# One PSUM pool instead of three, GpSimd's arithmetic on VectorE and ScalarE, and a new order in the last head and at the end

## The chip, the cores and the metric

The kernel runs on one core of a Trainium2 chip. The metric is the device time of one execution in microseconds (us), as the median of several runs. A profiled execution gives a trace as well, in which each instruction of each engine has a start and a duration. The engines are TensorE (PE; its weight loads are PEld), VectorE (DVE), ScalarE (ACT), GpSimd (POOL) and SyncE (SP), which only issues DMAs here.

## The reference

A decoder of two layers is run for one step, for a new sequence of 512 tokens and for 8 samples of 4 tokens each (544 columns in all, of width 1024). Layer 0 mixes with a short gated convolution, layer 1 with retention in 4 heads. All is in float32. Cut to what matters:

```
def swiglu(x, w_gate, w_up, w_down):
    return (jax.nn.silu(x @ w_gate) * (x @ w_up)) @ w_down

def retention_chunkwise(q, k, v, s0):          # chunks of 128 tokens
    def step(S, qkv):
        scores = jnp.einsum('bhid,bhjd->bhij', qc, kc) * decay
        inner = jnp.einsum('bhij,bhjv->bhiv', scores, vc)
        cross = jnp.einsum('bhid,bhdv->bhiv', qc, S) * cross_w[:, :, None]
        S_new = S * chunk_decay[:, None, None] + jnp.einsum('bhjd,bhjv->bhdv', kc * state_w[:, :, None], vc)
        return S_new, inner + cross

def trunk(x, ...):
    for i in range(DEPTH):
        h = rmsnorm(x, norm_mix[i])
        m, st = short_conv_mixer(...) if i % N_MIXERS == 0 else retention_mixer(...)
        x = x + m
        x = x + swiglu(rmsnorm(x, norm_ffn[i]), ffn_w_gate[i], ffn_w_up[i], ffn_w_down[i])
    return rmsnorm(x, final_norm), ...
```

In retention q and k are rotated by position, each head's output is normalized, multiplied with silu of a gate, and projected. The outputs are y and the states of both mixers.

## The kernel before

Activations lie with 128 features on the partitions and the 544 columns along the free side, in two halves of 272 (`HT`). So that TensorE can multiply at its faster type without losing float32 precision, each operand is split into a high and a low part: `split` (L180 on ScalarE writes the high part, L181 on VectorE subtracts it and leaves the low one). `project` (L167) then issues three matmuls for each tile of weights and half: high x high, low x high, high x low. The weights stream in through SP's queue into a pool of three buffers, and their split parts (`wh`, `wl`) into another of three.

The stages, with the places in the profile in us: the convolution (to 217), feed-forward 0 (217 to 592), retention with its four heads (595 to 1122) and feed-forward 1 (1122 to the end).

**Feed-forward.** The first two of eleven pairs of hidden tiles are plain products (`whole_pairs`). The others are `Job`s, one for the gate and one for the up side of a pair: `weights7` and `operands` form sums of quarter matrices, so that seven products (L422, 12 matmuls of 272 columns each) do the work of eight. The weight sums are L381 and L383 on GpSimd, L382 and L384 on VectorE; w, w2 and w4 are their buffers. A job holds three accumulators a, b and c; L482 on VectorE adds what `take` hands out (`c11`, `c22`, `c12`) to the partial sums in `g` and `u`. Product 3 goes into the same bank as product 5, so it can start only when the `c22` add has read that bank. Behind the up job the activations are multiplied (L581 on VectorE, L583 and L585 on GpSimd) and split (`xh`, `xl`). The order within a job is 1, then 6, 5, 2, 7, then the next job's 1, then 4 and 3. Three pairs make a group; behind it `down` multiplies with eight pieces of the third matrix and `residual` (L251) adds into `x`. A scheduler fills matmuls of the next job between the pieces of `down`.

**PSUM.** There are eight banks of 512 columns. The convolution and feed-forward 0 have a pool of eight single banks, retention one of two tiles of two banks (`mm`) with four single banks (`sm`), feed-forward 1 again one of eight. A new pool can be used only when the old one's last reader is through.

**Retention.** `qk_first` forms q and k of the first head, `qk_rotate` rotates (L812 to L817; L814 and L815 on GpSimd), `gated` normalizes and transposes (`yn` L970, transposes L987, product L990) and `out_project` splits the gated values (`yh`, `yl`) and multiplies them with eight output tiles. The next head's q and k products fill in while a head is finished; the last head has none, and `rest` there delays the second half of the columns.

**The end.** The last three tiles of x (`LATE`) are done half by half: `products(hf)`, then `scaled(hf)`, which forms the column statistics (L684 with `sqacc` and `sqlast`), `rN` (L209, L210), a diagonal (L690, L691), its product with ones (L693), the copy R (L694) and the outputs `ya` and `yb` (L698 to L701), and stores them. The sums of squares are `square_sum`: L204 on ScalarE, L205 on GpSimd, the last one L201.

Of the kernel before, what the change touches and what calls it, by code (L numbers as in the profile page):

```python
# [10 lines left out]
ALU = mybir.AluOpType  # L11
# [25 lines left out]
SKIP0 = 6  # L37

# [9 lines left out]
def hybrid_decode_kernel(ctx: ExitStack, tc: tile.TileContext, a: dict, o: dict):  # L48
# [19 lines left out]
    def bank1():  # L68
        return ps[0].tile([P, 512], F32, tag="mm", name=nm("mm"))

    def phase(stack, name, tiles, banks=2, skip=0):
        ps[:] = stack.enter_context(tc.tile_pool(name=name, bufs=tiles, space=bass.MemoryType.PSUM)), banks
        for _ in range(skip):
            bank1()
# [181 lines left out]
    c01 = ExitStack()  # L256
    phase(c01, "ps0", 8, 1, SKIP0)
# [113 lines left out]
    def weights7(src1, src2, sw):  # L371
# [9 lines left out]
        nc.gpsimd.tensor_tensor(s1, a21, a22, op=ALU.add)  # L381
        nc.vector.tensor_sub(s2, s1, a11)  # L382
        nc.gpsimd.tensor_tensor(a21, a11, a21, op=ALU.subtract)  # L383
# [20 lines left out]
    class Job:  # L404
# [23 lines left out]
        def begin(self):  # L428
            self.a = bank1()[:, :HT]
            self.product(self.a, 1, True)  # L430
            self.take("u1", self.a)

        def middle(self):
            for which in (5, 6) if self.lead else (6, 5):
# [3 lines left out]
                else:  # L438
                    self.c = bank1()[:, :HT]
                    self.product(self.c, 5, True)  # L440
            self.b = bank1()[:, :HT]
# [46 lines left out]
    def ffn(layer, next_gain):  # L488
        with ExitStack() as c1:
            if layer == 1:  # L490
                phase(ctx, "ps3", 8, 1, 4)
# [29 lines left out]
            def whole_pairs():  # L521
# [4 lines left out]
                for m in range(WHOLE):  # L526
# [20 lines left out]
                    for q in range(2):  # L547
                        d = tp.tile([P, 2, T], F32, tag="gu", name=nm("gu"))
                        gu.append(d)
                        for i in range(2):  # L550
                            each(lambda p, di, r: nc.vector.tensor_mul(di, p, r), pts[q][i], halves(d[:, i, :]), R)
                            if q == 0:
                                nc.scalar.activation(d[:, i, :], d[:, i, :], AF.Silu)
                            else:
                                nc.gpsimd.tensor_tensor(d[:, i, :], d[:, i, :], gu[0][:, i, :], op=ALU.mult)
# [5 lines left out]
            def gate_up(m):  # L561
# [16 lines left out]
                def up(what, src):  # L578
# [57 lines left out]
            made_in = MADE if layer == 0 else list(range(KT))  # L636
            whole = whole_pairs()
            groups = [list(range(m, min(m + GROUP, HJ))) for m in range(0, HJ, GROUP)]
# [15 lines left out]
            late = LATE if layer == 1 else 0  # L654
            down(last, made_in[: KT - late])
# [3 lines left out]
    def final(ms, acts, group_weights, fp, tp):  # L659
# [4 lines left out]
        def products(hf):  # L664
            c = slice(hf * HT, (hf + 1) * HT)
            for n in range(KT - LATE, KT):
                wh, wl = ws[n - KT + LATE]
                pt = [None, None]
                pt[hf] = bank1()
# [5 lines left out]
        def scaled(hf):  # L675
# [3 lines left out]
            pt = bank1()  # L679
# [38 lines left out]
    c01.close()  # L718


    with ExitStack() as c2:
        phase(c2, "ps2", 2)
        p1 = c2.enter_context(tc.tile_pool(name="ps2s", bufs=4, space=bass.MemoryType.PSUM))

        def bank():
            return p1.tile([P, 512], F32, tag="sm", name=nm("sm"))

# [50 lines left out]
        def qk_first(st):  # L778
# [26 lines left out]
        def qk_rotate(st, which, dt, pt):  # L805
# [8 lines left out]
            nc.gpsimd.tensor_tensor(t0, r[:, 1, :], sin, op=ALU.mult)  # L814
            nc.gpsimd.tensor_tensor(r[:, 1, :], r[:, 1, :], cos, op=ALU.mult)  # L815
# [84 lines left out]
        def state(h, st):  # L900
# [4 lines left out]
            for dt in range(2):  # L905
# [6 lines left out]
            for dt in range(2):  # L912
# [16 lines left out]
        def gate_project(h, st, n):  # L929
# [8 lines left out]
            nc.gpsimd.tensor_scalar_mul(g, g, g_ret(h * 4 + n))  # L938
# [109 lines left out]
        def out_project(h, st, rest=None):  # L1048
# [6 lines left out]
            def split_half(c):  # L1055
# [3 lines left out]
            if rest is None:  # L1059
                split_half(slice(0, T))  # L1060
            else:
                split_half(slice(0, HT))
            for n2 in range(4):
                wh, wl = load_piece(a["rtout"][h, n2], 2 * 4 * P)
                if n2 == 0 and rest is not None:
                    pts = [psum() for _ in range(2)]
                    for hf in range(2):
# [186 lines left out]
```

## Time and profile before

| | us |
|---|---|
| median of 3 runs | 1527.51 (1526.33 to 1528.83) |
| profiled execution | 1527.99 |
| its span, first to last instruction | 1525.9 |
| TensorE busy | 1482.7, 11008 matmuls |
| VectorE busy | 939.5, 1342 instructions |
| ScalarE busy | 550.1, 792 instructions |
| GpSimd busy | 340.7, 266 instructions |
| mean granted clock of TensorE | 0.993 |

A row of a timeline gives the start, the duration, engine, line, operation, output <- inputs and shape, the number of instructions taken together (xN), and in brackets the idle time ahead of it with what ended it. A row of waits gives the total, how often and the longest. A row of a window gives the stretch, its length, the busy us of the five engines with the number of instructions, the granted clock, the DMA share and GB/s.

### The profile page before, as it was taken

What the parts mean: (1) busy time and instruction counts of PE and PEld (TensorE: products, weight loads), DVE (VectorE), ACT (ScalarE), POOL (GpSimd) and SP (SyncE); (2) the same over time, 40 slices, a digit from 0 to 9 for tenths busy, and PEclk for the clock granted to TensorE, in tenths of its full rate; (3) what the DMA queues carried; (4) which work ended last, traced back from release to release, by engine and by line L of the source; (5) the groups of instructions that cost most, each with busy time, mean ns of one, the idle gap of its engine ahead of it and who ended that gap; (6) DMA issues with size and microseconds to landing.
All of it is one profiled execution on the core that took longest, in us unless ns stands there. A gap on an engine that the chain in (4) does not pass through costs nothing.

```text
span 1525.9 us, 26206 instructions
## 1 busy us (share of the span) xinstructions
PE 1482.7 (97%) x11008; PEld 1397.0 (92%) x11008; DVE 939.5 (62%) x1342; ACT 550.1 (36%) x792; POOL 340.7 (22%) x266
## 2 busy tenths in 40 slices
PE   8999999999999998999999999999999999999997
PEld 7999999999999998897987988989699999999996
DVE  5645439848658546647536734735749848748554
ACT  5222355525425334231232222113265525425333
POOL 2000234304214112212102202201134313314113
PEclk9999999999999999999999999999999999999998
DMA  5222273223222226237235423713474223232222
GB/s 203 88 93 84 93 175 98 95 83 98 83 98 98 73 80 194 73 113 260 70 125 179 167 77 109 251 47 111 166 176 101 87 93 98 80 101 92 79 79 74
DMA packets 69462, 173.37 MB, mean 114 GB/s; under 512 B 6480, under 2 KB 22992, under 8 KB 69344
## 3 DMA queue, kind: packets, MB, share of 16 engines
q1 hardware_dynamic: 66432, 162.12, 32.0%
q0 software_dynamic: 2336, 8.46, 3.3%
q8 instruction: 86, 1.41, 0.4%
q10 hardware_dynamic: 576, 1.11, 0.2%
q14 instruction: 32, 0.26, 0.1%
HBM read 150.50 MB, written 21.18 MB: 113 GB/s over the span
## 4 chain that ended last, share of the span: by engine, by line
PE 76%; DVE 10%; issue 5%; POOL 4%; ACT 2%; DMA 1%; DVEq 0%; SPq 0%; ACTq 0%; POOLq 0%
PE mm L167 48%; PE mm L422 15%; DVE wl L181 3%; PE sm L838 2%; PE sm L839 2%; PE sm L840 2%; PE sm L1027 1%; ACT h L180 1%; DVE x L251 1%; PE sm L155 1%; PE sm L157 1%; DVE g L482 1%; POOL w L383 1%; POOL rot L815 1%; PE sm L156 1%
## 5 line engine op out<-in xcount | busy, mean ns | idle before, releaser
L180 ACT ACTIVATE wh<-w 128x1024 fp32r<-128x1024 f32 (+2 forms) x235 | 228.0, 974 | 515.1 <-PE mm L167 388.6
L167 PE MATMUL mm<-xh,wh 128*128 128x272 f32 x1760 | 373.6, 293 | 16.2 <-ACT wh L180 10.9
L167 PE MATMUL mm<-xh,wl 128*128 128x272 f32 x1760 | 367.0, 290 | 1.7 <-DVE wl L181 1.0
L167 PE MATMUL mm<-xl,wh 128*128 128x272 f32 x1760 | 364.6, 288 | 0.0
L181 DVE TENSOR_TENSOR wl<-w,wh 128x1024 fp32r<-128x1024 f32 (+2 forms) x235 | 294.3, 1257 | 39.9 <-ACT wh L180 38.5
L167 PEld LDWEIGHTS mm<-xh,wh 128*128 128x128 f32 x1760 | 276.8, 190 | 29.6 <-ACT wh L180 16.7
L167 PEld LDWEIGHTS mm<-xh,wl 128*128 128x128 f32 x1760 | 276.1, 189 | 4.7 <-DVE wl L181 4.3
L167 PEld LDWEIGHTS mm<-xl,wh 128*128 128x128 f32 x1760 | 277.4, 189 | 0.0
L251 DVE TENSOR_TENSOR x<-x,mm 128x272 f32<-128x272 f32 (+1 forms) x170 | 77.2, 487 | 199.1 <-PE mm L167 198.7
L422 PE MATMUL mm<-oh,wh 128*128 128x272 f32 x576 | 166.4, 289 | 0.0
L422 PE MATMUL mm<-oh,wl 128*128 128x272 f32 x576 | 166.3, 289 | 0.0
L422 PE MATMUL mm<-ol,wh 128*128 128x272 f32 x576 | 166.2, 289 | 0.0
L422 PE MATMUL mm<-oh,h 128*128 128x272 f32 x432 | 126.1, 292 | 6.5 <-DVE g L482 5.3
L422 PE MATMUL mm<-oh,l 128*128 128x272 f32 x432 | 124.8, 289 | 0.0
L381 POOL TENSOR_TENSOR w<-w 128x512 f32<-128x512 f32 x36 | 48.8, 1356 | 339.3 <-DMA w<-in_ffgu_dram 166.3
L422 PE MATMUL mm<-ol,h 128*128 128x272 f32 x432 | 124.5, 288 | 0.0
L422 PEld LDWEIGHTS mm<-oh,wh 128*128 128x128 f32 x576 | 108.6, 189 | 0.4 <-ACT u L479 0.4
L422 PEld LDWEIGHTS mm<-oh,wl 128*128 128x128 f32 x576 | 108.6, 189 | 0.0
L422 PEld LDWEIGHTS mm<-ol,wh 128*128 128x128 f32 x576 | 108.5, 188 | 0.0
L938 POOL TENSOR_SCALAR gate<-gate,vec 128x544 f32<-128x544 f32 x16 | 32.1, 2008 | 275.7 <-ACT gate L937 275.7
L181 DVE TENSOR_TENSOR l<-w,h 128x1024 fp32r<-128x1024 f32 x72 | 77.5, 1076 | 22.6 <-ACT h L180 21.9
L422 PEld LDWEIGHTS mm<-oh,h 128*128 128x128 f32 x432 | 81.4, 188 | 9.7 <-DVE g L482 7.5
(224 smaller groups left out, 2395.8 us busy)
## 6 DMA issues: line engine op xcount, KB each, us to landing
w<-in_ffgu_dram SPq DMA_DIRECT2D x88, 512.0 KB, 3.5
w<-in_ffdn_dram SPq DMA_DIRECT2D x96, 192.0 KB, 2.5
S<-in_rets_dram SPq DMA_DIRECT2D x16, 1024.0 KB, 7.3
out_rets_dram<-S SPq DMA_DIRECT2D x16, 1024.0 KB, 5.3
w<-in_cvin_dram SPq DMA_DIRECT2D x21, 512.0 KB, 3.5
w<-in_rtqk_dram SPq DMA_DIRECT2D x16, 512.0 KB, 3.5
w<-in_rtv_dram SPq DMA_DIRECT2D x16, 512.0 KB, 3.6
w<-in_rtg_dram SPq DMA_DIRECT2D x16, 512.0 KB, 4.0
```

Of the source, the lines that this page charges most:

```text
L155: nc.tensor.matmul(out, lh, rh, start=start, stop=False)
L156: nc.tensor.matmul(out, lh, rl, start=False, stop=False)
L167: nc.tensor.matmul(half(pt, hf)[:, :HT], w[:, c], act[k][:, hf * HT : (hf + 1) * HT], start=(first and k == ks[0] and i == 0), stop=(last ...
L180: nc.scalar.activation(dh, src, AF.Copy)
L181: nc.vector.tensor_sub(dl, src, dh.bitcast(F32))
L251: last_residual[0] = nc.vector.tensor_add(xk, xk, p)
L381: nc.gpsimd.tensor_tensor(s1, a21, a22, op=ALU.add)
L422: nc.tensor.matmul(out, w[:, c], b[k][:, at, :], start=(first and k == 0 and i == 0), stop=(k == n - 1 and i == 2), skip_group_check=True,)
L838: nc.tensor.matmul(out, xh[kt][:, ts_], wh[:, cw], start=(kt == 0), stop=False)
L839: nc.tensor.matmul(out, xh[kt][:, ts_], wl[:, cw], start=False, stop=False)
L840: nc.tensor.matmul(out, xl[kt][:, ts_], wh[:, cw], start=False, stop=(kt == KT - 1))
L938: nc.gpsimd.tensor_scalar_mul(g, g, g_ret(h * 4 + n))
```

## The change

One pool `ps` serves all phases: two tiles of two banks (`mm`, written m below) and four single banks (`sm`, written s; a pair of them makes one tile). `wide` sets in which order `psum()` hands out m and s. Jobs and statistics take single banks with `bank()`. L381, L383, L583, L585, the product in `whole_pairs` and two products of the rotation go from GpSimd to VectorE; the gate's scale goes to ScalarE. In the last head the state is formed in two halves of its rows (`dts`), the second one ahead of `out_project`, and the two gated steps are handed to it as a list. `out_project` cycles m, m, s. At the end the second half's products all stand ahead of the first half's outputs. Most lines behind L66 have a number that is one higher in the new kernel, and six lower from `qk_first` on (L251 is L252, L693 is L694, L987 is L981).

```diff
-    ps = [None, 2]
+    ps = ctx.enter_context(tc.tile_pool(name="ps", bufs=2, space=bass.MemoryType.PSUM))
+    kinds, at = ["m"], [0]
+    def wide(kind):
+        kinds[0], at[0] = kind, 0
     def psum():
-        if ps[1] == 1:
-            return [bank1(), bank1()]
-        return ps[0].tile([P, 2, 512], F32, tag="mm", name=nm("mm"))
+        kind = kinds[0][at[0] % len(kinds[0])]
+        at[0] += 1
+        if kind == "s":
+            return [bank(), bank()]
+        return ps.tile([P, 2, 512], F32, tag="mm", name=nm("mm"), bufs=2)
+    def bank():
+        return ps.tile([P, 512], F32, tag="sm", name=nm("sm"), bufs=4)
...
-        nc.gpsimd.tensor_tensor(s1, a21, a22, op=ALU.add)
+        nc.vector.tensor_add(s1, a21, a22)
         nc.vector.tensor_sub(s2, s1, a11)
-        nc.gpsimd.tensor_tensor(a21, a11, a21, op=ALU.subtract)
+        nc.vector.tensor_sub(a21, a11, a21)
...
                     elif what == "c22":
-                        nc.gpsimd.tensor_tensor(u[:, 1, HT:], u[:, 1, HT:], g[:, 1, HT:], op=ALU.mult)
+                        nc.vector.tensor_mul(u[:, 1, HT:], u[:, 1, HT:], g[:, 1, HT:])
                     elif what == "c12":
-                        nc.gpsimd.tensor_tensor(u[:, 0, :], u[:, 0, :], g[:, 0, :], op=ALU.mult)
+                        nc.vector.tensor_mul(u[:, 0, :], u[:, 0, :], g[:, 0, :])
...
+            wide("mmss")
             whole = whole_pairs()
+            wide("m")
...
             late = LATE if layer == 1 else 0
+            wide("mms")
             down(last, made_in[: KT - late])
...
         next(first)
-        next(second)
-        next(first, None)
         drain(second)
+        drain(first)
         drain(scaled(1))
...
-                    project(pt, wh, wl, 0, xh, xl, first, not first, ks=part, weave=iter(()) if first else steps)
+                    project(pt, wh, wl, 0, xh, xl, first, not first, ks=part, weave=iter(()) if first and pt is pts[0] else steps)
...
-            nc.gpsimd.tensor_tensor(t0, r[:, 1, :], sin, op=ALU.mult)
-            nc.gpsimd.tensor_tensor(r[:, 1, :], r[:, 1, :], cos, op=ALU.mult)
+            nc.vector.tensor_mul(t0, r[:, 1, :], sin)
+            nc.vector.tensor_mul(r[:, 1, :], r[:, 1, :], cos)
...
-            nc.gpsimd.tensor_scalar_mul(g, g, g_ret(h * 4 + n))
+            nc.scalar.activation(g, g, AF.Copy, scale=g_ret(h * 4 + n))
...
+            split_gated(slice(0, HT if rest else T))
+            wide("mms")
             for n2 in range(4):
                 wh, wl = load_piece(a["rtout"][h, n2], 2 * 4 * P)
+                pts = []
+                for n in range(2):
+                    pts.append(psum())
+                    if n2 == 0 and rest:
+                        rest[n]()
+                        project(pts[n], wh, wl, n * 4 * P, yh, yl, hfs=(0,))
+                    else:
+                        project(pts[n], wh, wl, n * 4 * P, yh, yl)
+                        residual(2 * n2 + n, pts[n])
...
-                        state(h, st)
+                        state(h, st, (0,))
...
             else:
-                out_project(h, st, rest)
+                state(h, st, (1,))
+                out_project(h, st, [lambda: gated(h, st, yn, 3), lambda: gated(h, st, yns, 4)])
```

The scheduler's order of instructions moves with it. VectorE, in the middle of a gate job of feed-forward 0, before (`mm_577` is the bank of products 5 and 3, the first add into it `c22`, the second `c12`):

```order
L482 TENSOR_TENSOR g_564_5094<-g_564_5094,mm_578_5179 128x272
L181 TENSOR_TENSOR wl_574_5146<-w_565_5127,wh_573_5145 128x1024
L482 TENSOR_TENSOR g_564_5094<-g_564_5094,mm_577_5166 128x272
L382 TENSOR_TENSOR w2_583_5252<-w2_583_5252,w_582_5251 128x512
L181 TENSOR_TENSOR wl_586_5261<-w_582_5251,wh_585_5260 128x1024
L181 TENSOR_TENSOR l4_576_5150<-w4_568_5130,h4_575_5149 128x512
L482 TENSOR_TENSOR g_564_5094<-g_564_5094,mm_577_5166 128x272
L384 TENSOR_TENSOR w4_584_5253<-w_582_5251,w2_583_5252 128x512
```

The same place on VectorE in the new kernel (the bank is `sm_533`, `c11` reads `sm_534`):

```order
L182 TENSOR_TENSOR wl_530_5064<-w_521_5045,wh_529_5063 128x1024
L482 TENSOR_TENSOR g_520_5012<-g_520_5012,sm_534_5097 128x272
L482 TENSOR_TENSOR g_520_5012<-g_520_5012,sm_533_5084 128x272
L381 TENSOR_TENSOR w2_539_5170<-w_537_5168 128x512
L382 TENSOR_TENSOR w2_539_5170<-w2_539_5170,w_538_5169 128x512
L383 TENSOR_TENSOR w_537_5168<-w_538_5169,w_537_5168 128x512
L182 TENSOR_TENSOR wl_542_5179<-w_538_5169,wh_541_5178 128x1024
L182 TENSOR_TENSOR l4_532_5068<-w4_524_5048,h4_531_5067 128x512
L482 TENSOR_TENSOR g_520_5012<-g_520_5012,sm_533_5084 128x272
L384 TENSOR_TENSOR w4_540_5171<-w_538_5169,w2_539_5170 128x512
```

The `wl` that stood between the `c11` and the `c22` add stands ahead of both, and L381 and L383 have come in behind them.

TensorE, in a down group of feed-forward 0 at the start of a new weight piece, before (`mm_637` and `mm_642` with their second halves are down pieces, `mm_627` is a bank of the next job):

```order
L167 MATMUL mm_637_5681<-xh4_82,wl_636_5678 128x272
L167 MATMUL mm_638_5682<-xh4_82,wl_636_5678 128x272
L422 MATMUL mm_627_5581<-oh_224_2270,l2_620_5515 128x272
L167 MATMUL mm_642_5728<-xh2_80,wh_640_5724 128x272
L167 MATMUL mm_643_5729<-xh2_80,wh_640_5724 128x272
```

And the new kernel's TensorE at the third piece of the same group (`mm_596` is the piece, `sm_583` and `sm_629` belong to the next job):

```order
L168 MATMUL mm_592_5597<-xl4_93,wh_590_5593 128x272 x2
L168 MATMUL mm_592_5597<-xh4_85,wl_591_5594 128x272 x2
L422 MATMUL sm_583_5499<-oh_201_2230,l2_576_5433 128x272
L422 MATMUL sm_629_5944<-oh_198_2227,h2_575_5432 128x272
L422 MATMUL sm_629_5944<-ol_202_2231,h2_575_5432 128x272
L422 MATMUL sm_629_5944<-oh_198_2227,l2_576_5433 128x272
L422 MATMUL sm_629_5944<-oh_199_2228,h2_575_5432 128x272
L422 MATMUL sm_629_5944<-ol_203_2232,h2_575_5432 128x272
L168 MATMUL mm_596_5642<-xh2_83,wh_594_5638 128x272 x2
```

Six matmuls of the job now stand where one stood, between the last use of one piece's weights and the first use of the next.

TensorE in the last head, before (`sm_1317` is attention output, L987 are transposes of `yn`, L167 the output projection):

```order
L155 MATMUL sm_1317_11002<-vh_1252_10550,sh_1269_10693 128x512
L156 MATMUL sm_1317_11002<-vl_1253_10551,sh_1269_10693 128x512
L157 MATMUL sm_1317_11002<-vh_1252_10550,sl_1270_10694 128x512
L987 MATMUL sm_1322_11024<-cb_64,yn_1313_10985 128x128 x4
L167 MATMUL mm_1332_11055<-yh_1327_11039,wh_1330_11050 128x272
L167 MATMUL mm_1333_11056<-yh_1327_11039,wh_1330_11050 128x272
L987 MATMUL sm_1334_11081<-cb_64,yn_1321_11022 128x128 x4
L987 MATMUL sm_1335_11087<-cb_64,yn_1326_11037 128x128 x3
```

The new kernel's TensorE ahead of the output projection (`mm_1274` is the second half of the state's rows):

```order
L156 MATMUL mm_1274_10919<-vh_1200_10445,knh_1187_10362 128x512
L157 MATMUL mm_1274_10919<-vl_1201_10446,knh_1187_10362 128x512
L158 MATMUL mm_1274_10919<-vh_1200_10445,knl_1188_10363 128x512
L168 MATMUL mm_1281_10951<-yh_1276_10935,wh_1279_10946 128x272
L168 MATMUL mm_1281_10951<-yl_1277_10936,wh_1279_10946 128x272
L168 MATMUL mm_1281_10951<-yh_1276_10935,wl_1280_10947 128x272
L168 MATMUL mm_1281_10951<-yh_1276_10935,wh_1279_10946 128x272
L981 MATMUL sm_1282_10952<-cb_67,yn_1268_10902 128x128 x4
```

Twelve matmuls of the state stand in place of the bare step from the transposes to the output projection.

More of the change, by code (lines that the diff above doesn't have):

```diff
@@ L428, in begin @@
         def begin(self):
-            self.a = bank1()[:, :HT]
+            self.a = bank()[:, :HT]
             self.product(self.a, 1, True)
@@ L668, in products @@
                 pt = [None, None]
-                pt[hf] = bank1()
+                pt[hf] = bank()
                 project(pt, wh, wl, 0, ah, al, hfs=(hf,))
@@ L678, in scaled @@
             yb = tp.tile([P, 4, HT], F32, tag="gu", name=nm("yb"))
-            pt = bank1()
+            pt = bank()
             mq = pt[:, 496:499]
@@ L711, in final @@
         next(first)
-        next(second)
-        next(first, None)
         drain(second)
+        drain(first)
         drain(scaled(1))
     ffn(0, lambda kt: g_mix(1, kt))
-    c01.close()
     with ExitStack() as c2:
[L722 to L726, printed above, removed]
+        wide("m")
         tp = c2.enter_context(tc.tile_pool(name="rt", bufs=2))
@@ L898, in keys, with state @@
             st["kn"] = (knh, knl, k2)
-        def state(h, st):
+        def state(h, st, dts=(0, 1)):
             knh, knl, k2 = st["kn"]
@@ L904, in state @@
             pt = psum()
-            for dt in range(2):
+            for dt in dts:
                 for jt in range(4):
@@ L911, in state @@
                     )
-            for dt in range(2):
+            for dt in dts:
                 so = tp.tile([P, DV], F32, tag="yn", name=nm("so"), bufs=2)
@@ L1053, in out_project, with split_gated @@
             yl = [yll[:, n, :] for n in range(4)]
-            def split_half(c):
+            def split_gated(c):
                 for n in range(4):
                     split(yh[n][:, c], yl[n][:, c], st["gate"][:, n, c])
[L1059 to L1062, printed above, removed]
+            split_gated(slice(0, HT if rest else T))
+            wide("mms")
             for n2 in range(4):
                 wh, wl = load_piece(a["rtout"][h, n2], 2 * 4 * P)
-                if n2 == 0 and rest is not None:
-                    pts = [psum() for _ in range(2)]
-                    for hf in range(2):
-                        if hf == 1:
-                            rest()
-                            split_half(slice(HT, T))
-                        for n in range(2):
-                            project(pts[n], wh, wl, n * 4 * P, yh, yl, hfs=(hf,))
+                pts = []
[7 more added lines that the diff above has]
+                        residual(2 * n2 + n, pts[n])
+                if n2 == 0 and rest:
+                    split_gated(slice(HT, T))
                     for n in range(2):
+                        project(pts[n], wh, wl, n * 4 * P, yh, yl, hfs=(1,))
                         residual(n, pts[n])
-                    continue
-                for n in range(2):
-                    pt = psum()
-                    project(pt, wh, wl, n * 4 * P, yh, yl)
-                    residual(2 * n2 + n, pt)
+            wide("m")
         st = qk_start(0)
@@ L1115, in hybrid_decode_kernel @@
                     else:
-                        state(h, st)
+                        state(h, st, (0,))
             yns = normalized(st["po"])
-            def rest():
-                gated(h, st, yn, 3)
-                gated(h, st, yns, 4)
             if more:
```

20 lines of the change are left out of this document (5 added, 15 removed).

## The prediction

> **What bounds the kernel now.** I read the page's busy times first, then the list of what TensorE waited for, then the timelines around each of those waits on the engine that is named.
>
> ```profile
> PE 1482.7 (97%) x11008; PEld 1397.0 (92%) x11008; DVE 939.5 (62%) x1342; ACT 550.1 (36%) x792; POOL 340.7 (22%) x266
> ```
>
> TensorE is busy for 1482.7 of 1525.9 us. The change issues the same matmuls, so a gain can come only from the 43.2 us in which TensorE sits idle, or from stretches in which its clock is low. The waits behind that idle time, on TensorE alone:
>
> ```profile
> PE mm L167 <- ACT wh L180: 10.9, 7, 7.5
> PE mm L167 <- DVE x L251: 7.1, 4, 4.0
> PE mm L422 <- DVE g L482: 5.3, 10, 1.0
> PE mm L693 <- DVE sqacc L691: 2.6, 2, 1.9
> PE mm L167 <- ACT yh L180: 2.5, 2, 1.7
> PE mm L684 <- POOL sqacc L205: 1.3, 1, 1.3
> PE mm L422 <- DVE u L482: 1.1, 2, 0.5
> PE mm L167 <- DVE wl L181: 1.0, 6, 0.2
> PE mm L167 <- ACT wh L185: 0.9, 1, 0.9
> PE sm L987 <- DVE yn L970: 0.9, 2, 0.6
> PE sm L238 <- DVE sqlast L233: 0.8, 1, 0.8
> PE mm L684 <- ACT sqlast L201: 0.7, 1, 0.7
> ```
>
> (Columns: total us, times, longest.) These rows add up to 35.1 us. 7.5 of them are the first load at the start, which the change does not touch; some 27.6 us in the middle are what it can win, and the tail behind the last matmul makes up the rest. I take the places one by one, by the kernel's stages.
>
> **A: the feed-forward jobs.** Product 3 adds into the bank that the `c22` add (L482) still has to read. It waits 5.3 + 1.1 = 6.4 us in twelve places. One of them:
>
> ```profile
> 472.29 2.19 DVE L181 TENSOR_TENSOR wl<-w,wh 128x1024 fp32r<-128x1024 f32 x1
> 472.11 1.29 POOL L381 TENSOR_TENSOR w<-w 128x512 f32<-128x512 f32 x1 [2.98 <-DVE l L181]
> 473.48 2.16 POOL L383 TENSOR_TENSOR w<-w,w 128x512 f32<-128x512 f32 x1
> 464.87 1.23 DVE L181 TENSOR_TENSOR wl<-w,wh 128x1024 fp32r<-128x1024 f32 x1 [0.16 <-ACT wh L180]
> 474.88 0.39 PE L422 MATMUL mm<-oh,h 128*128 128x272 f32 x1 [0.44 <-DVE g L482]
> ```
>
> The `c22` add stands on VectorE behind a `wl` subtraction. That instruction takes 1.23 us while GpSimd is silent, and 2.19 us while GpSimd runs L381 or L383: the two slow each other down. The costs for one gate and up pair of jobs (21.77 us), grouped:
>
> ```profile
> 460.12:481.89 21.77, 21.33 (x169) 21.11 (x168) 19.27 (x22) 11.83 (x20) 9.39 (x6) 1.00 0.32 111
> L181 DVE TENSOR_TENSOR wl<-w,wh 128x1024 fp32r<-128x1024 f32 x4 | 6.8, 1708 | 0.5 <-ACT wh L180 0.5
> L181 DVE TENSOR_TENSOR l<-w,h 128x1024 fp32r<-128x1024 f32 x3 | 3.7, 1225 | 2.3 <-ACT h L180 2.3
> L382 DVE TENSOR_TENSOR w<-w,w 128x512 f32<-128x512 f32 x2 | 2.9, 1428 | 0.0
> L384 DVE TENSOR_TENSOR w<-w,w 128x512 f32<-128x512 f32 x2 | 2.5, 1266 | 0.0
> L181 DVE TENSOR_TENSOR xl<-u,xh 128x544 fp32r<-128x544 f32 x2 | 1.4, 724 | 0.2 <-ACT xh L180 0.2
> L181 DVE TENSOR_TENSOR l<-w,h 128x512 fp32r<-128x512 f32 x2 | 1.4, 689 | 0.1
> L581 DVE TENSOR_TENSOR u<-mm,g 128x272 f32<-128x272 f32 x1 | 0.4, 428 | 0.0
> ```
>
> The first row is the window (TensorE, weight load, VectorE, ScalarE, GpSimd busy us); VectorE is at 19.27 of 21.77. The change puts six more instructions on it: L381 and L383 twice each, in the shape of the 689 ns row, so 4 x 0.69 = 2.76, and the two products at 0.43 and 0.72, together 3.91 us. What goes is the slowing down: wl 4 x (1.71 - 1.23) = 1.9, L382 2 x (1.43 - 0.69) = 1.5, L384 2 x (1.27 - 0.69) = 1.2, together 4.6 us. VectorE so ends at about 19.27 + 3.9 - 4.6 = 18.6 us a pair, against 169 x 0.126 = 21.3 us on TensorE: it stays the faster one. In the new order `c22` follows `c11` directly and the `wl` stands ahead of both, so the add is earlier by the whole subtraction, 1.2 to 2.2 us, and the longest wait was 1.0. New in VectorE's queue is that L381 waits for a weight load; L382 waited for the same pair of loads before, and behind GpSimd's 1.29 us, so nothing behind it comes later than now. I take 5.5 of 6.4 us; bounds 0 (the add stays behind something else) and 6.4. The rotations of retention lose GpSimd's two products each to VectorE at 0.72 each, and the gate's scale goes to ScalarE, which is busy 36%; both are covered by TensorE except in D.
>
> The Trainium skill, page "SBUF — State Buffer", section "Who interferes with whom", says that a VectorE instruction with two SBUF inputs contends with a GpSimd instruction that reads SBUF, and that the later one blocks completely until the other is done. The trace agrees that they contend, with a loss (0.96 us) smaller than either GpSimd instruction it met (1.29 and 2.16), so "completely" is not shown; by the full rule the saving would be up to 9.39 us a pair instead of 4.6, which changes nothing as long as TensorE is the longer.
>
> **B: the down groups.** At the start of each of six groups the second or third weight piece is split late:
>
> ```profile
> 519.52 0.84 ACT L180 ACTIVATE wh<-w 128x768 fp32r<-128x768 f32 x1 [5.25 <-PE mm L167]
> ```
>
> ScalarE was idle for 5.25 us and waited for a buffer that TensorE still read: of three buffers the next job holds two, and the matmuls of that job which fill in behind had run out (one single matmul is left ahead of the new piece). The waits: 10.9 - 7.5 = 3.4 us on `wh` and 1.0 on `wl`, 4.4 in all. With a single PSUM pool the down pieces use the two-bank tiles and the jobs the single banks, and the order has 6 job matmuls (0.75 us) for that one ahead of each of the next four pieces, and two ahead of the fifth. The waits on `wh` were 3.4 / 6 = 0.57 us each, so that is enough; for the last pieces it is not sure. I take 3.5; bounds 0 and 4.4.
>
> **C: into retention.** A new PSUM pool can be opened only when the last residual add has read the old one:
>
> ```profile
> 591.00 0.77 DVE L251 TENSOR_TENSOR x<-x,mm 128x272 f32<-128x272 f32 x2
> 594.62 0.77 DVE L251 TENSOR_TENSOR x<-x,mm 128x272 f32<-128x272 f32 x2
> 595.53 0.79 PE L167 MATMUL mm<-xh,wh 128*128 128x272 f32 x2 [3.98 <-DVE x L251]
> 595.50:601.50 6.00, 5.97 (x26) 6.00 (x27) 3.52 (x14) 1.22 (x2) 0.00 (x0) 0.50 0.90 295
> ```
>
> The first tile will need only the add of 591.00, the second that of 594.62, with 24 matmuls (3.0 us) between: 0.3 + 0.6 us stay of 3.98. The idle time has a second price: for six us behind it the granted clock is 0.50, and 26 matmuls take 5.97 us for 26 x 0.126 = 3.3, so 2.7 us more. The 0.8 on `sqlast` goes too, since the statistics start a half earlier; but two value matmuls instead of fourteen now cover the first rotation, which I put at 0.75 us. C: 4.0 + 2.7 + 0.8 - 1.7 = 5.8; bounds 2 (the clock still drops) and 7.5.
>
> The Trainium skill, page "TensorE: Matmul & The Clock Gate", part 1, says the clock halves after an idle window of about 3.4 us and needs a busy one to come back. The trace agrees here (3.98 us, then 0.50); in E below the clock falls with no single gap over 1.7 us, so there the trace is stricter than the rule. By the rule the gaps left in C keep the clock; by E's row they might not, which is the bound of 2.
>
> **D: the output projection** of heads 0 to 2 has two PSUM tiles, and the third product waits for a residual add:
>
> ```profile
> 735.59 0.72 DVE L817 TENSOR_TENSOR rot<-rot,rt 128x544 f32<-128x544 f32 x1 [1.25 <-POOL rot L815]
> 736.24 0.71 DVE L251 TENSOR_TENSOR x<-x,mm 128x544 f32<-128x544 f32 x1
> 737.00 0.52 PE L167 MATMUL mm<-yh,wh 128*128 128x272 f32 x2 [1.04 <-DVE x L251]
> ```
>
> The add stands in VectorE's order behind the end of a rotation that waits for GpSimd. Three such waits: 7.1 - 4.0 = 3.1 us. A third tile gives each add one more product (48 matmuls, 6 us), and the GpSimd step ahead of it is gone. I take 3.0; bounds 0 and 3.1.
>
> **E: the last head** has nothing to fill the gated products with: 2.5 us on `yh` and 0.9 on `yn`.
>
> ```profile
> 1092.90 0.78 PE L167 MATMUL mm<-yh,wh 128*128 128x272 f32 x2 [1.66 <-ACT yh L180]
> 1093.00:1097.00 4.00, 3.70 (x18) 3.31 (x19) 3.53 (x7) 0.81 (x3) 0.60 (x2) 0.58 0.11 41
> ```
>
> In the four us behind, the clock is 0.58: 3.70 x 0.42 = 1.55 us more. Half of the state's matmuls (12 at the 0.23 us of 512 columns, 2.8 us) move into the 1.66. The chain behind the last `yn` (transposes, gating, split) is then covered by nine matmuls only, 1.1 us, so I leave 1.2 standing: 3.4 + 1.55 - 1.2 = 3.7; bounds 1 and 4.9. Two state stores move with it behind SP's earlier work; nobody waits for them.
>
> **F: into the second feed-forward** goes the other new pool: 0.9 us, as its slot comes free a tile earlier; bounds 0 and 0.9.
>
> **G: the end.** All products of the second half now stand ahead of the first half's outputs:
>
> ```profile
> 1510.17 0.73 PE L693 MATMUL mm<-sqacc,ones 128*128 128x272 f32 x2 [0.76 <-DVE sqacc L691]
> 1512.19 1.72 DVE L701 SCALAR_TENSOR_TENSOR yb<-x,vec,mm 128x272 f32<-128x272 f32 x4
> 1513.68 0.38 PE L684 MATMUL mm<-cb,sqacc 128*128 128x1 f32 x2 [1.28 <-POOL sqacc L205]
> 1517.91 1.27 PE L693 MATMUL mm<-sqacc,ones 128*128 128x272 f32 x2 [1.86 <-DVE sqacc L691]
> ```
>
> The wait ahead of the first L693 is filled by one product (12 matmuls, 1.5 us from 1509.4), so the first half's L693 starts near 1510.9 for 1510.2. The sums for the second half on GpSimd, then ScalarE come ahead of the first half's outputs, so the second statistics need not wait for them and start near 1512.2 for 1513.7. But then `rN`, the next step, stands on VectorE behind six L701 (6 x 0.43 = 2.6 us from about 1511.8), so it is done near 1514.4; of the 1.5 won at the statistics and some 0.7 of waiting inside them, 1.7 stay. The half's output stores on ScalarE's and SP's queues move about 1 us back, and the second half's stand behind them. Bounds -2 (the two halves' outputs collide) and 2.5.
>
> **The sum**: 5.5 + 3.5 + 5.8 + 3.0 + 3.7 + 0.9 + 1.7 = 24.1 us. The profiled execution took 1527.99 us, 2.1 outside the span: 1525.9 - 24.1 + 2.1 = 1503.9, and as this execution stands 0.5 above the median of the runs (1527.51), I predict 1503.5.
>
> **Rivals.**
> 1. VectorE becomes the bound of the job pairs. This needs the slowing down not to come from GpSimd: then 19.27 + 3.91 = 23.2 us a pair stands against 21.3, 1.9 more for each of 18 pairs, 34 us lost against the 18.6 won outside A: about 1527.5 - 18.6 + 34 = 1543, slower. It decides from 21.3 + 18.6 / 18 = 22.3 us of VectorE a pair. Against it: 1.23 and 2.19 in the same instruction, by GpSimd's state. Chance 5%.
> 2. Half of it: A's and B's waits find another late producer (a weight load now at the head of VectorE's queue, one of four single banks not yet read), and 9.0 us stay: 1512.5. If C and E trip the clock again as well, 4 more: 1516.5. For it: 2.35 us of VectorE idle in a pair, on ScalarE, show that its order is tight. 20%.
> 3. The change does not do what it says: the banks' new split gives as many waits as it takes, in the whole pairs and the conv projection, which have few in the list now; 24 us come back, within 3 us (0.2%) of before, about what a measurement of this kernel can tell from no change. 6%.
> 4. All of the middle goes, and the clock's losses with it: 27.6 + 2.7 + 1.55 = 31.9 us, less 3 that the end keeps: 1498.5 and down to 1497. 7%.
>
> My own forecast, 1499 to 1510, has the remaining 62%. The range from 1498 to 1519 takes in rival 2 and leaves the two tails of 1 and 3. Faster 0.89, same 0.05, slower 0.06 by these cases.
>
> **What would show it.** A: no TensorE wait on L482 left, `wl` at 1.23 us throughout, VectorE at 18 to 19 us in a pair. B: no wait on `wh` over 0.2 us but the first. C: no gap over 1 us and a clock of 1.00 where retention starts. D: no residual add named by TensorE. E: two waits under 0.8 us near 1070 to 1080, clock over 0.9. G: the last L694 about 8.1 us behind the first half's statistics, for 10.3. Wrong it would be if a pair of jobs takes over 21.5 us, or if the list of waits names L381, L382 or the banks of L422.

## The result, and the profile after

The changed kernel takes 1492.06 us (median of 4 runs, 1491.29 to 1493.29) against 1527.72 of the kernel before on the same chip: a ratio of 0.9768, 95% interval [0.9751, 0.9785]. That is 35.7 us faster, where 24.1 were forecast; the time lies below the range. The direction and the places were right, the size was not.

The profile after has a span of 1490.7 us. Its busy times:

```profile
PE 1471.2 (99%) x11008; PEld 1392.7 (93%) x11008; DVE 919.5 (62%) x1400; ACT 565.9 (38%) x805; POOL 93.8 (6%) x118
```

And the list of what TensorE waited for (total us, times, longest):

```profile
PE mm L168 <- ACT wh L181: 6.7, 1, 6.7
PE sm L694 <- DVE sqacc L692: 2.4, 1, 2.4
PE sm L832 <- ACT wh L181: 0.9, 1, 0.9
PE sm L685 <- POOL sqacc L206: 0.8, 1, 0.8
PE sm L981 <- DVE yn L964: 0.6, 3, 0.2
PE mm L168 <- ACT yh L181: 0.5, 1, 0.5
PE mm L168 <- DVE x L252: 0.3, 1, 0.3
```

No L422 stands in it any more, and no `wh` but the first load's and one in the value product. TensorE issues the same 11008 matmuls, yet it is busy for 11.5 us less. The idle time fell from 43.2 us to 19.5, so it explains 23.7 of the 35.2 us of span; the rest is in the "busy" column.

To see where, the span is cut at the same matmuls of both traces, from start to start (us; the 9.0 forecast for A and B are put down half to each layer):

| stage | before | after | change | forecast |
|---|---|---|---|---|
| start to the first job matmul (L422) | 255.35 | 255.78 | +0.4 | 0 |
| first to last job matmul, layer 0 (A, B) | 312.46 | 302.05 | -10.4 | -4.5 |
| from there to the first value product (C) | 46.87 | 41.04 | -5.8 | -5.8 |
| first value products of head 0 to those of head 3 (D) | 397.66 | 393.94 | -3.7 | -3.0 |
| from there to the statistics of feed-forward 1 (E, F) | 116.75 | 113.13 | -3.6 | -4.6 |
| from there to the first job matmul | 44.31 | 44.31 | 0.0 | 0 |
| first to last job matmul, layer 1 (A, B) | 312.34 | 302.03 | -10.3 | -4.5 |
| last job matmul to the first end statistics | 20.66 | 20.66 | 0.0 | 0 |
| from there to the last product with ones (G) | 12.12 | 10.32 | -1.8 | -1.7 |
| tail | 7.41 | 7.41 | 0.0 | 0 |

All rows but those of the two job stages stand within 1 us of the forecast. The two job stages gave 20.7 us for 9.0: that is 11.7 us, the whole of the miss. The first row moves by up to 1.3 us between the traces (254.5 to 255.8 over all kernels here), and nothing is read from it.

VectorE in a pair of jobs, as the prediction reckoned it, first the window (another pair than the prediction's, of layer 0 too):

```profile
363.57:385.30 21.73, 21.73 (x175) 21.73 (x174) 18.26 (x28) 12.12 (x21) 0.00 (x0) 1.00 0.31 106
```

and the groups of instructions in it (count, busy us, mean ns of one, idle before):

```profile
L182 DVE TENSOR_TENSOR wl<-w,wh 128x1024 fp32r<-128x1024 f32 x4 | 4.9, 1222 | 0.9 <-ACT wh L181 0.9
L382 DVE TENSOR_TENSOR w<-w,w 128x512 f32<-128x512 f32 x2 | 1.4, 688 | 0.0
L381 DVE TENSOR_TENSOR w<-w 128x512 f32<-128x512 f32 x2 | 1.4, 682 | 0.0
L383 DVE TENSOR_TENSOR w<-w,w 128x512 f32<-128x512 f32 x2 | 1.4, 682 | 0.0
```

With GpSimd silent (0.00) `wl` takes 1222 ns for 1708 and L382 688 for 1428. VectorE holds more instructions than before and is busy for less: 18.26 us where 18.6 were worked out. TensorE has no idle time left in the window.

### The profile page after: what moved, and what is told of

It reads as the page before. It is cut to its first block, busy times and chain, and to the rows that moved or that the text cites. A ratio compares the mean times of both kernels' runs of the same rounds, so it can differ in the third digit from the quotient of the medians.

```text
span 1490.7 us, 25998 instructions
## 1 busy us (share of the span) xinstructions
PE 1471.2 (99%) x11008; PEld 1392.7 (93%) x11008; DVE 919.5 (62%) x1400; ACT 565.9 (38%) x805; POOL 93.8 (6%) x118
## 3 DMA queue, kind: packets, MB, share of 16 engines
q8 instruction: 86, 1.41, 0.4%
q10 hardware_dynamic: 576, 1.11, 0.2%
## 4 chain that ended last, share of the span: by engine, by line
PE 95%; DVE 3%; issue 1%; ACT 1%; POOL 0%; DMA 0%; DVEq 0%; SPq 0%; POOLq 0%; ACTq 0%
PE mm L168 43%; PE sm L422 26%; PE sm L168 11%; PE sm L832 2%; PE sm L833 2%; PE sm L834 2%; PE sm L1021 1%; PE sm L156 1%; PE sm L158 1%; PE sm L157 1%; PE mm L1034 1%; DVE wl L182 1%; PE mm L839 1%; PE mm L156 1%; PE sm L981 1%
## 5 line engine op out<-in xcount | busy, mean ns | idle before, releaser
L252 DVE TENSOR_TENSOR x<-x,mm 128x544 f32<-128x544 f32 x86 | 61.9, 720 | 170.1 <-PE mm L168 170.1
L422 PE MATMUL sm<-oh,wl 128*128 128x272 f32 x576 | 166.5, 289 | 0.0
L422 PE MATMUL sm<-oh,wh 128*128 128x272 f32 x576 | 166.5, 289 | 0.0
L422 PE MATMUL sm<-ol,wh 128*128 128x272 f32 x576 | 166.3, 289 | 0.0
L422 PE MATMUL sm<-oh,l 128*128 128x272 f32 x432 | 124.7, 289 | 0.0
L422 PE MATMUL sm<-ol,h 128*128 128x272 f32 x432 | 124.7, 289 | 0.0
L422 PE MATMUL sm<-oh,h 128*128 128x272 f32 x432 | 124.6, 288 | 0.0
L422 PEld LDWEIGHTS sm<-oh,wh 128*128 128x128 f32 x576 | 108.7, 189 | 0.4 <-ACT u L479 0.4
L422 PEld LDWEIGHTS sm<-oh,wl 128*128 128x128 f32 x576 | 108.7, 189 | 0.0
L422 PEld LDWEIGHTS sm<-ol,wh 128*128 128x128 f32 x576 | 108.5, 188 | 0.0
L182 DVE TENSOR_TENSOR l<-w,h 128x1024 fp32r<-128x1024 f32 x72 | 68.7, 955 | 35.7 <-ACT h L181 35.5
L422 PEld LDWEIGHTS sm<-ol,h 128*128 128x128 f32 x432 | 81.4, 188 | 0.0
L422 PEld LDWEIGHTS sm<-oh,l 128*128 128x128 f32 x432 | 81.4, 188 | 0.0
```

The lines of the kernel that those rows point to most:

```text
L182: nc.vector.tensor_sub(dl, src, dh.bitcast(F32))
L252: last_residual[0] = nc.vector.tensor_add(xk, xk, p)
L422: nc.tensor.matmul(out, w[:, c], b[k][:, at, :], start=(first and k == 0 and i == 0), stop=(k == n - 1 and i == 2), skip_group_check=True,)
```

## What was open

Theory 1: a wait costs more than the idle time that the profile shows for it. A matmul of 272 columns is shown for 0.29 us, but the next one starts 0.126 us behind it. So the first 0.163 us of any wait lie beneath the shown end of the matmul ahead, and shorter waits show nothing. Theory 2: with GpSimd silent, TensorE itself runs faster everywhere. Beside this, each step had its own question: whether it was the contention or the order on VectorE that made the waits of A, and whether the fall of the clock in C and E came from the waits.

The rows of the kernel before already had the answer, one wait of A on TensorE:

```profile
276.90 0.29 PE L422 MATMUL mm<-oh,wl 128*128 128x272 f32 x1
277.72 0.39 PE L422 MATMUL mm<-oh,h 128*128 128x272 f32 x1 [0.53 <-DVE u L482]
277.94 0.29 PE L422 MATMUL mm<-ol,h 128*128 128x272 f32 x1
278.07 0.29 PE L422 MATMUL mm<-oh,l 128*128 128x272 f32 x1
```

The starts are 0.82 and 0.22 us apart where 0.13 is the rule. The wait cost 0.69 + 0.10 = 0.79 us, and 0.53 are shown. The 0.10 is in the next spacing: the first matmul behind a wait is shown for 0.39 us instead of 0.29.

## The experiments

### e1: GpSimd's work moved, nothing else

In the kernel before:

```diff
-        nc.gpsimd.tensor_tensor(s1, a21, a22, op=ALU.add)
+        nc.vector.tensor_add(s1, a21, a22)
...
-            nc.gpsimd.tensor_scalar_mul(g, g, g_ret(h * 4 + n))
+            nc.scalar.activation(g, g, AF.Copy, scale=g_ret(h * 4 + n))
```

and likewise the other six that the change moves.

> The kernel before with GpSimd's sums and products moved to VectorE and ScalarE, and nothing else. Theory 1 (a wait of TensorE costs 0.16 us more than the idle time shown, since a matmul is shown for 0.29 us and the next can start after 0.126; waits under 0.16 us show no idle time at all): the twelve waits on c22 go with 6.4 us of idle time and 8.5 us of start-to-start time, perhaps 1 to 3 us in D; the down groups and the PSUM boundaries stay. 1516 to 1519 us, and the time between the first and last job matmul of a layer falls by 4.2 to 5.5 us of 312.4. Theory 2 (GpSimd's silence lets TensorE run faster everywhere): the whole unexplained 10 us of the two job stages comes with the moves: 1508 to 1511 us, and the usual spacing of matmuls falls below 0.1256 us.

Measured: 1512.45 us, ratio 0.9898 [0.9883, 0.9913], 15.9 us faster than before. The waits that stay:

```profile
PE mm L167 <- ACT wh L180: 10.1, 7, 6.7
PE mm L167 <- DVE x L251: 4.0, 1, 4.0
PE mm L167 <- ACT yh L180: 2.4, 2, 1.6
```

All twelve waits on L482 are gone, and the job stages take 307.17 and 307.19 us, 5.3 and 5.2 less: within theory 1's 4.2 to 5.5 and half of what theory 2 asks. The spacing of matmuls that wait for nothing stays at 0.126 us, where theory 2 wanted less. The total does not decide: it lies 3.6 us below theory 1's range and 1.5 above theory 2's. D gave more than the 1 to 3 us allowed for: of the four waits on the residual only the one of C is left, and the stage from head to head fell by 4.4 us. So GpSimd's moves alone take away D's waits, most likely its two products in the rotation, which the prediction's rows show ahead of the add; the third tile is not needed for that. B, E and F stay as they were.

Two more things differ. C takes 45.73 us for 46.87 and the end 13.11 for 12.12, though their waits are those of the kernel before: the same 3.98 us ahead of retention are followed by a mean clock of 0.72 over six us, where it was 0.50, and at the end the clock is 0.53 from 1498 to 1500 us, during the statistics, where it was 1.00 before. What a wait costs in clock so is not the same each time. And the scheduler's order moved along: in ten of the 18 gate jobs, the very ten that waited before, `c22` now follows `c11` directly, as in the new kernel. So e1 has both cures of A and cannot part contention from order.

### e2: one pool, the new last head and the new end, with GpSimd's work back

In the changed kernel, the edit of e1 the other way round.

> The changed kernel with all of GpSimd's sums and products put back on GpSimd; one pool, the last head and the end stay as changed. Theory 1: waits of the down groups stay gone; if the c22 waits come back, they cost 8.5 us start to start, so 1500 to 1504 us; if the order keeps c22 ahead of the weight sums, 1493 to 1497 us. Either way the loss equals the idle time shown plus 0.16 us a wait, plus short waits that show nothing. Theory 2: 1506 to 1510 us whatever the list of waits shows.

Measured: 1502.96 us, ratio 0.9837 [0.9821, 0.9853]. Eleven of the twelve waits of A are back. The list has three more rows that the kernel after lacks, of 0.2 to 0.4 us each; the rows of A are:

```profile
PE sm L422 <- DVE g L482: 4.8, 10, 1.0
PE sm L422 <- DVE u L482: 0.5, 1, 0.5
```

The job stages take 307.03 and 306.17 us. B's and D's waits stay gone, so the pool gives all of B: 5.4 and 6.2 us a layer against the kernel before, or 5.2 a layer as what e1 leaves of the whole, from a listed 4.4 us for both layers. In e2 and the kernel before alike the spacing of matmuls that wait for nothing is 0.126 us, as in the kernel after, and the time lies in theory 1's range, 3 us under theory 2's. Theory 2 falls: GpSimd's silence did not make TensorE's matmuls come closer together.

### e3 and e6: half of GpSimd's work back

e3, in the changed kernel:

```diff
-        nc.vector.tensor_add(s1, a21, a22)
+        nc.gpsimd.tensor_tensor(s1, a21, a22, op=ALU.add)
...
-        nc.vector.tensor_sub(a21, a11, a21)
+        nc.gpsimd.tensor_tensor(a21, a11, a21, op=ALU.subtract)
```

> The changed kernel with only the two weight sums L381 and L383 back on GpSimd. VectorE's wl goes back to 1.7 us on average and L382 and L384 to 1.3 to 1.4. If the contention made the c22 waits (my prediction's step A), they come back: 1500 to 1503 us. If it was the place of c22 in VectorE's order (here it still follows c11 directly), the 1.2 us of slack cover the contention: 1491.5 to 1494 us. Theory 2: about 1500 us with no waits to show for it.

e6, in the changed kernel:

```diff
-                        nc.vector.tensor_mul(u[:, 1, HT:], u[:, 1, HT:], g[:, 1, HT:])
+                        nc.gpsimd.tensor_tensor(u[:, 1, HT:], u[:, 1, HT:], g[:, 1, HT:], op=ALU.mult)
...
-                        nc.vector.tensor_mul(u[:, 0, :], u[:, 0, :], g[:, 0, :])
+                        nc.gpsimd.tensor_tensor(u[:, 0, :], u[:, 0, :], g[:, 0, :], op=ALU.mult)
```

> The changed kernel with only the two products behind the up job (c22 and c12 with the gate) back on GpSimd; the weight sums stay on VectorE. Its order on VectorE has a wl subtraction between the c11 and the c22 add again. If c22's place in the order makes the waits on product 3: six a layer come back, 4.2 us a layer start to start, 1499 to 1502 us in all. If contention made them: GpSimd has two short instructions a pair only, 1492.5 to 1494.5 us.

Measured: e3 1493.84 us (0.9777 [0.9763, 0.9792]), e6 1491.72 us (0.9767 [0.9753, 0.9782]), which is the changed kernel's time and 0.8 us below the lower of e6's two ranges. VectorE at the same gate job, first of e2, then of e6, then of e3:

```profile
366.43 0.43 DVE L482 TENSOR_TENSOR g<-g,sm 128x272 f32<-128x272 f32 x1
366.77 2.17 DVE L182 TENSOR_TENSOR wl<-w,wh 128x1024 fp32r<-128x1024 f32 x1
368.88 0.42 DVE L482 TENSOR_TENSOR g<-g,sm 128x272 f32<-128x272 f32 x1
```

```profile
363.57 0.43 DVE L482 TENSOR_TENSOR g<-g,sm 128x272 f32<-128x272 f32 x1
363.92 1.22 DVE L182 TENSOR_TENSOR wl<-w,wh 128x1024 fp32r<-128x1024 f32 x1
365.05 0.43 DVE L482 TENSOR_TENSOR g<-g,sm 128x272 f32<-128x272 f32 x1
```

```profile
363.55 2.31 DVE L182 TENSOR_TENSOR wl<-w,wh 128x1024 fp32r<-128x1024 f32 x1
365.79 0.77 DVE L482 TENSOR_TENSOR g<-g,sm 128x272 f32<-128x272 f32 x2
```

In e2, as before, both the contention (2.17) and the bad order (`wl` between `c11` and `c22`) are there, and TensorE waits. e6 has the bad order without contention: no wait, 302.09 and 302.05 us. e3 has the contention without the bad order in this job (both adds in one row, behind `wl`): 302.85 and 303.21 us. It is the same in all ten gate jobs that waited: `wl` stands between the two adds in each of them in e6, in none of them in e3. So there a wait needed both, and either cure suffices nearly alone. Neither of the two single causes that I set against each other, in e3 and in e6, was the whole of it. e3 also shows short waits that nearly escape the view: the stages are 0.8 and 1.2 us longer, and no L422 stands in its list of waits, which leaves out idle times of up to 0.15 us.

### e4 and e5: a late first tile in retention

e4 asks for a tile at the start of retention and leaves it (one line, `psum()`); e5 writes one column of it, which nobody reads:

```diff
+            skipped = psum()
+            nc.tensor.matmul(half(skipped, 0)[:, :1], ident, mean_w[:, 0:1], start=True, stop=True)
             pts = [psum() for _ in ws]
```

> The changed kernel with one PSUM tile skipped at the start of retention, so that the first product waits for the last residual add (584.9 us in the profile after) instead of the one before it. Idle time of about 3.3 us comes back there. If the clock falls behind it as in the kernel before (0.50 for 6 us): 2.7 us more, in all +5.6 us: 1497.7 us. If the clock's fall has nothing to do with the wait: +3.0 us: 1495.0 us, clock 1.00.

> The changed kernel, in which one PSUM tile at the start of retention is written with one column that nobody reads, so that the first product gets the tile whose last reader is the last residual add (at 584.2 to 584.9 us in the profile after). About 3.3 us of idle time come back there (3.5 start to start), less the 0.5 that the second tile waited. If the clock falls behind it, as the prediction's step C has it: 2.5 to 2.7 us more, 5.6 us in all: 1497.7 us and a clock near 0.50 for some 5 us. If the clock's fall in the kernel before had another cause: +3.0 us, 1495.1 us, clock 1.00.

Measured: e4 1491.61 us (0.9761 [0.9747, 0.9776]), with the trace of the changed kernel at that place: a tile that is never written holds no one up, and the run says nothing on the clock. e5: 1494.19 us (0.9784 [0.9769, 0.9798]), and stage C takes 44.27 us for 41.04. The wait that came is another than I meant, statistics ahead of the products, and at 1.95 us it is shorter than the 3.3 I planned, so the time is below both of my figures; but a wait is there. TensorE's row in the timeline, then the windows behind it:

```profile
583.00 0.38 PE L225 MATMUL sm<-cb,sqacc 128*128 128x1 f32 x2 [1.95 <-POOL sqacc L206]
```

```profile
584.00:586.00 2.00, 2.00 (x13) 2.00 (x13) 2.00 (x12) 1.30 (x2) 0.00 (x0) 0.67 0.86 277
586.00:588.00 2.00, 2.00 (x11) 2.00 (x10) 1.80 (x4) 0.00 (x0) 0.00 (x0) 0.50 0.89 307
```

Eleven products run at full clock behind it, and only then, 1.4 us after the first of them, the clock falls to 0.50 for about 3.4 us: fifteen matmuls stand 0.227 us apart for 0.126, which is 1.5 us of the 3.2 lost. With the tile free in time the clock stays at 1.00 there, so the clock's part of C was a price of the wait, as step C had it.

### e7 and e8: the last head and the end

e7 forms the last head's state whole, as before; e8 has the old order of the end:

```diff
-                        state(h, st, (0,))
+                        state(h, st)
...
-                state(h, st, (1,))
```

```diff
         next(first)
+        next(second)
+        next(first, None)
         drain(second)
-        drain(first)
```

> The changed kernel with the last head's state formed whole, where the kernel before formed it, so that nothing stands between the last attention product and the output projection. By the prediction's step E: about 2 us of idle time and 0.3 to 0.5 of hidden time come back, and the clock falls again for 2 to 4 us (1 to 1.5 us): +3 to +4 us, 1495 to 1496 us. If the list of two gated steps and the order around it, not the state's twelve matmuls, made the gain: within 1 us of the changed kernel.

> The changed kernel with the end in the old order (one product of the second half behind the first half's outputs). By the prediction's step G: +1.8 us between the first statistics and the last product with ones, 1493.9 us. If the gain there came from the other parts: no difference.

Measured: e7 1493.64 us (0.9778 [0.9761, 0.9794]), e8 1493.64 us (0.9779 [0.9765, 0.9794]). In e7 the last head's stage takes 115.67 us for 113.13, and the clock falls again there, 0.50 in one window of two us:

```profile
1072.00:1074.00 2.00, 0.40 (x3) 0.30 (x2) 1.53 (x7) 0.79 (x3) 0.61 (x2) 0.98 1.03 382
1074.00:1076.00 2.00, 1.54 (x8) 1.15 (x8) 2.00 (x4) 0.60 (x2) 0.43 (x1) 0.50 0.15 56
```

That is 2.5 us, less than the 3 to 4 I expected but well over the other case's 1, and most of the 3.6 that E and F gave: the state's twelve matmuls are most of it. In e8 the end takes 12.11 us for 10.32: 1.8, as expected to a tenth. Both medians, 1.6 us above the changed kernel's, lie inside the interval of the ratio; it is the stage times of the traces that carry these two readings.

### e9: waits of known size

Behind the changed kernel's last output stand rounds of one matmul, whose result ScalarE copies for the next round, and m more that don't depend on it (`fresh` is a copy on ScalarE, `stretch(t, m)` issues m matmuls, `HT` is 272):

```diff
+        for m in range(10, 0, -1):
+            for r in range(12):
+                d = bank()
+                nc.tensor.matmul(d[:, :HT], xh[0][:, :P], t, start=True, stop=True)
+                nxt_t = fresh(d[:, :HT], 1e-3)
+                stretch(t, m)
+                t = nxt_t
...
+        for k in range(1, 10):
+            d = bank()
+            nc.tensor.matmul(d[:, :HT], xh[1][:, :P], t, start=True, stop=True)
+            t = fresh(d[:, :HT], 1e-3)
+            for _ in range(k - 1):
+                t = fresh(t.bitcast(F32))
+            stretch(t, 96)
```

> The changed kernel, with a measurement of its own behind its last output (its time is that much longer, some 350 us). Part 1: 12 rounds each of one matmul, whose result ScalarE copies to be the next round's operand, and m further matmuls behind it, m from 10 down to 1, all 128x272 on TensorE. With a chain of about 0.9 us, TensorE must wait for less and less time as m grows. Theory 1 (idle time shown is the true wait less 0.16 us): at each m the time of a round is (m+1) x 0.126 plus the idle time shown plus 0.16 us, and there is an m (6 or 7) at which rounds are longer than (m+1) x 0.126 with no idle time shown. Theory 2 (idle time shown is the whole wait): a round is (m+1) x 0.126 plus the idle shown. Part 2: stretches of 96 matmuls (12 us) parted by one wait behind k ScalarE copies, k from 1 to 9, so waits of about 0.7 to 3.5 us. If the clock falls behind a wait as short as the 1.9 us of e5, it stays 1.00 up to k = 3 or 4 and is 0.50 for about 3.4 us behind longer ones, not always at the same length; if only waits of over 3 us count, up to k = 7.

Measured (a profiled execution, 1785.15 us with the addition): the chain from one such matmul to the next is 0.88 us. TensorE's rows for m = 6, then 4, then 3:

```profile
1568.01 0.29 PE L1147 MATMUL sm<-t,xh 128*128 128x272 f32 x1
1568.14 0.92 PE L1140 MATMUL sm<-t,xh 128*128 128x272 f32 x6
1568.90 0.28 PE L1147 MATMUL sm<-t,xh 128*128 128x272 f32 x1
...
1589.06 0.39 PE L1147 MATMUL sm<-t,xh 128*128 128x272 f32 x1
1589.29 0.66 PE L1140 MATMUL sm<-t,xh 128*128 128x272 f32 x4
1589.94 0.39 PE L1147 MATMUL sm<-t,xh 128*128 128x272 f32 x1
...
1600.50 0.40 PE L1147 MATMUL sm<-t,xh 128*128 128x272 f32 x1
1600.74 0.54 PE L1140 MATMUL sm<-t,xh 128*128 128x272 f32 x3
1601.39 0.39 PE L1147 MATMUL sm<-t,xh 128*128 128x272 f32 x1
```

All three rounds take 0.88 us. With seven matmuls that is 7 x 0.126, and nothing is lost. With five, 0.63 us of work takes 0.88, and no idle time is shown at all: rows touch, the next one starting at 1589.94 where the shown ones end at 1589.29 + 0.66 = 1589.95. With four, 0.38 us is lost and 0.11 shown (1600.74 + 0.54 = 1601.28 to 1601.39). The medians over the rounds:

| m | work (m+1) x 0.1256 | round | lost | idle shown | difference |
|---|---|---|---|---|---|
| 6 | 0.879 | 0.879 | 0.00 | 0 | 0 |
| 5 | 0.754 | 0.880 | 0.13 | 0 | 0.13 |
| 4 | 0.628 | 0.881 | 0.25 | 0 | 0.25 |
| 3 | 0.502 | 0.880 | 0.38 | 0.11 | 0.27 |
| 2 | 0.377 | 0.881 | 0.50 | 0.24 | 0.27 |

So theory 1 holds, with a larger figure than I gave it: a wait costs 0.27 us more than it shows, 0.16 beneath the end of the matmul ahead and 0.105 in the longer spacing behind. The chain alone sets the length of these rounds, so the table shows how much loss goes unseen; that the longer spacing costs the kernel itself time is seen from its own spacings, below. (At m = 1 the granted clock is 0.68; that row is left out.)

In part 2 the waits are 0.55, 1.01, 1.41, 1.87, 2.33, 2.79, 3.25, 3.71 and 4.17 us of idle time. The first five leave the clock alone; the last four are followed by 16, 15, 12 and 24 matmuls at 0.227 us for 0.126. The bound so lies between 2.33 and 2.79 us here, between the two cases that I had set; each length was tried once. The first wait that did it, with the windows behind it and behind the 2.33:

```profile
1714.97 1.33 PE L1140 MATMUL sm<-t,xh 128*128 128x272 f32 x5 [2.79 <-ACT t L1134]
```

```profile
1699.50:1703.00 3.50, 3.22 (x25) 3.22 (x26) 0.00 (x0) 0.23 (x1) 0.00 (x0) 1.00 0.00 0
1714.70:1718.20 3.50, 3.23 (x15) 3.23 (x16) 0.00 (x0) 0.22 (x1) 0.00 (x0) 0.57 0.00 0
```

The Trainium skill, page "TensorE: Matmul & The Clock Gate", part 1, gives one idle window of about 3.4 us as the condition. Here the clock fell behind shorter ones: 2.79 us in e9, and 1.95 in e5, where one-column matmuls stand around the wait.

## Why the prediction was right or wrong, point by point

**A and B, wrong in size.** The step that failed is the one that read the cost of a wait off the list of waits: 6.4 us for A and 4.4 for B, of which I took 5.5 and 3.5, 9.0 in all. The runs put 20.7 us in their place: 10.4 for A by e1, and 10.3 for B as what is left. Behind it stands the sentence that a gain can come only from TensorE's idle time or from a low clock: the busy time fell by 11.5 us, more than the 2.7 and 1.55 of C's and E's clock, because the shown end of a matmul covers the start of a wait. In layer 0, 19 waits show idle time in the job stage, 6.0 us in all. The matmuls behind them start 9.1 us later than the spacing of 0.126 would have it (0.161 hidden in each, 3.1 in all); and of spacings between 0.20 and 0.26 us, as they follow a wait, there are 39 before and 25 after: 14 fewer, worth 1.5 more. 9.1 + 1.5 = 10.6 for the 10.4 us measured; layer 1 gives 9.0 + 1.4 = 10.4 for 10.3, and the waits of e2, counted the same way, 9.1 for 9.1. Beside this hidden share (4.6 and 4.4 us), I had kept back 1.8 us for waits that might stay, and none stayed, and the list left out 1.1 us of idle time that the timeline has. These come to 11.9 us for the 11.7.

The mechanism was right for both: the contention went (e6), the place of `c22` helps when it is there (e3), and with the pool the filling matmuls no longer run out in B (e2). Half of it was not known from the trace alone: that either of A's two cures would do. One reading was too weak, without a change to the sum: the `wl` shown there started 0.18 us behind L381, so only 1.11 us of L381 were left, and it lost 0.96; L383 then had 1.00 us of that `wl` ahead of it and took 2.16, where the shortest L383 in the trace takes 1.28. Each so waited for nearly the whole rest of the other, and "completely" is closer than the prediction put it.

**C, right, to the tenth by luck**: 5.8 of 5.8. (The same wait cost 1.1 us less in e1.) The 1.7 that I left standing show as 0.3 and 0.9 us of idle time with their hidden shares, and the clock is back at 1.00 there; in e5 about half of the loss was the clock's.

**D, right in sum, wrong in part**: 3.7 for 3.0; 3.1 of idle time and three times 0.2 hidden. I named the third tile and GpSimd's step together; e1 and e2 show that GpSimd's moves and the tile each do it alone, 4.4 us in e1 and 3.3 in e2.

**E and F, one us too high**: 3.6 for 4.6. Waits of 0.5 and 0.1 us stay in the last head, with the hidden share on each. e7 confirms the twelve matmuls and the clock for 2.5 of it.

**G, right**: 1.8 for 1.7, and by the steps given: the wait ahead of the first L694 is gone, the second statistics start 5.8 us behind the first where it was 7.3, and `rN` stands behind six L702. The sign named for G (8.1 us for 10.3) fits no rows: from the first statistics to the last product with ones it is 10.3 us for 12.1. The two rows of VectorE:

```profile
1479.23 1.72 DVE L702 SCALAR_TENSOR_TENSOR yb<-x,vec,sm 128x272 f32<-128x272 f32 x4
1480.87 0.15 DVE L210 TENSOR_SCALAR rN<-sm 128x3 f32<-128x3 f32 x1
```

**The rivals.** VectorE did not become the bound: 18.26 us a pair, against the 22.3 at which that would have decided. Rival 4, all of the middle gone, was the nearest, and even its 31.9 us, before the 3 it kept for the end, was too little, since it added up the same column. The range was cut off below at a sum of idle times, which is no bound.

## What to carry to other kernels

Cost a wait of TensorE by the distance of matmul starts, not by the idle time shown: here each wait costs up to 0.27 us more than the view says (0.24 on average in layer 0's jobs), and a wait under that shows as nothing. Many short waits weigh more than their sum in the list; a bound "all idle time gone" is too small by their number times that share. When two causes must meet for a wait (a slowed instruction and a bad place in the queue), curing either is enough, so test them one by one before paying for both; and look at the order of instructions in each test, since the scheduler moves it along with the edit.

## What the runs showed of the hardware that was not expected

A matmul of 128x272 behind a wait is followed by a spacing of 0.23 us instead of 0.126, and is itself shown for 0.39 us instead of 0.29, at full clock (e9, m = 2 to 5). The clock can fall behind an idle time of 1.95 us (e5), stays at 2.33 and falls at 2.79 (e9), and then stays low for 12 to 24 matmuls of 272 columns, 2.7 to 5.4 us. While it is at 0.50 these matmuls start 0.227 us apart, 1.8 times the usual 0.126. The fall need not come with the wait: in e5 it set in 1.4 us after work had begun again, and the same 3.98 us of idle time cost 1.1 us less in e1 than in the kernel before.
